# Exponentials written over the logits in PSUM, with a copy for GpSimd's sum

## The chip, the cores and the metric

The kernel runs on one core of a Trainium2 chip. A core has TensorE (PE, matmuls), VectorE (DVE), ScalarE (ACT), GpSimd (POOL) and SyncE (SP, which issues the DMAs). They run side by side, each through its own queue in order, and wait for each other by semaphores. SBUF is the working memory that all of them reach; PSUM holds what matmuls write, and of the other engines only VectorE and ScalarE read or write it. The metric is the device time of one execution in microseconds. Profiles count from the first to the last instruction, the span.

## What is computed

One layer that mixes three groups of heads over 2048 positions of width 1024: forgetting attention (6 heads of 64), a chunked mLSTM (4 heads of 96), and cross-attention to 256 memory tokens (4 heads of 64). All take their inputs from one projection, go through a gate and an output projection, and a layer norm ends it. The change touches the two attentions:

```python
logits = einsum('bhqd,bhkd->bhqk', q_blk, kh) + c_blk[..., :, None] - c[..., None, :]
p = softmax(where(causal, logits, -inf), axis=-1)
return einsum('bhqk,bhkd->bhqd', p, vh)
```

In the cross-attention the logits are `q @ mem_k` alone, without a mask.

## The kernel before, in words

*Precision.* Matmuls run in a rounded 32-bit format (`F32R`). To keep more digits, a value `x` is split into a rounded `h` and the rest `l = x - h`. A projection is three matmuls for each piece of 128 rows (`h,h`, `l,h` and `h,l`), and the weights of attention, which are exponentials, are split as well: `ph` is rounded, `pl` the rest, and each is multiplied by the values `v`.

*Attention.* An item is one head with a block of 512 queries; there are 40. `att_max` finds each query's largest logit: matmuls into a PSUM tile `mx`, and VectorE's maxima of it into `mp`. `att_qk` makes the logits, 128 keys at a time (a chunk): two matmuls into a PSUM tile `st`, `st<-qm,km` and `st<-qb,kb`, the keys on the partitions and up to 512 queries along them, with the maximum already subtracted. Items of the second half of the positions have 12 or 16 chunks, others 2, 4 or 8. There are 272 chunks in all. `att_exp` (lines 604 to 624) then does for each chunk:

- ScalarE writes `ph`, the rounded exponential of `st`
- ScalarE writes `p`, the full exponential of `st`, to SBUF; `st` is free then
- VectorE writes `pl = p - ph`
- GpSimd adds `p` to the item's sum `acc` over the chunks (the softmax's denominator); the item's first chunk has no addition, its `p` is `acc` itself

`att_pv` multiplies: `o<-ph,v` and `o<-pl,v`, both adding into one PSUM tile `o`. `att_end` divides by the sum and stores the block.

*Around it.* TensorE's other work fills in between: the projections (`pj<-h,h`, `pj<-l,h`, `pj<-h,l`, listed in `SEQ`), later the mLSTM units (`ml_unit`, 16 of them, tile names `mq`, `mk`, `vv`, `dd`, `cst`, `vw`, `kr`) and the output tiles (`out_tile`, `pj<-h,yh` and so on), for which the output weights `wo` are loaded.

*What sets the order.* The class `Machine` is a planner. Each part of the work is a generator that asks for buffers (`Alloc`) and yields instructions. The planner keeps a clock for each engine by costs of its own, and issues next, on the engine that can start earliest, the ready instruction with the lowest number in `PRIO`. So the order on each engine is fixed when the program is made, and a change of a few lines can move instructions everywhere behind it. Buffers are counted by tag: two of `st`, two of `p`, two of `ph`, three of `pl`, one of `o`; `ph` and `pl` can also use the four of `ta`. The loader of weights has the lowest number of all and takes a `raw` buffer or, where none is free, a `p` (`RAW`).

Nearly all instructions are recorded by the planner's `issue`, so the profile puts them on line 204 and they are told apart by the names of their tiles.

## Time and profile before

| | |
|---|---|
| time, median of 3 runs | 1445.92 us (1445.73 to 1448.08) |
| the profiled execution | 1446.53 us, its span 1444.8 us |
| granted clock of TensorE, mean | 0.987 |
| attention's logits | from 74 us to 1124 us of the span |
| last projection, first output matmul | 1172 us, 1189 us |
| HBM read and written | 97.62 MB and 44.00 MB, 98 GB/s over the span |

A row of a group reads: line, engine, operation, tiles written and read, shapes, count | busy us, mean ns of one | idle time of the engine just before them and what ended it. The mean ns is the length of one instruction. Where instructions follow each other without a wait, the next begins before the one before it ends, so their pitch is shorter than that length. A row of a timeline has the start, the length, the engine and the instruction. PEld is the loading of a matmul's weights, which runs beside the matmul before it.

### The profile page before, as it was taken

The numbers are of one execution on the slowest core, as the hardware profiler recorded it, in microseconds if no ns is written. First come the engines' busy times: TensorE is split into PE (matmuls) and PEld (weight loads), VectorE is DVE, ScalarE is ACT, GpSimd is POOL, SyncE is SP. The second block draws the span as 40 slices with busy tenths as digits, with TensorE's granted clock in tenths as the row PEclk, the third lists the DMA queues.
The fourth block names the chain that finished last, engine by engine and source line by source line (L and its number), as shares of the span: only waits on it lengthen the run. The fifth ranks groups of instructions, "written<-read, shape, count | busy, mean of one in ns | idle before, by whom it ended". The sixth has DMA issues, their size and how long they took to land.

```text
span 1444.8 us, 22963 instructions
## 1 busy us (share of the span) xinstructions
PE 1355.7 (94%) x7904; PEld 1160.5 (80%) x7904; DVE 1058.8 (73%) x2158; ACT 673.1 (47%) x1463; POOL 435.0 (30%) x401
## 2 busy tenths in 40 slices
PE   6999999999999999999999989999998969989998
PEld 6888998998877798977787768787686757877886
DVE  5887356637588979579797788779889786767455
ACT  5444234424355643344646364544636566555100
POOL 2011002303043201013737071722726314445300
PEclk9999999999999999999999999999999979999999
DMA  6613232231322452431011402131111586765432
GB/s 200 205 46 103 79 109 86 78 115 56 116 74 74 143 177 61 131 105 54 21 49 53 121 9 61 38 104 56 58 40 56 165 239 200 216 185 160 134 134 92
DMA packets 123556, 151.81 MB, mean 105 GB/s; under 512 B 16832, under 2 KB 72080, under 8 KB 123440
## 3 DMA queue, kind: packets, MB, share of 16 engines
q1 hardware_dynamic: 123440, 150.35, 34.9%
q8 instruction: 63, 1.03, 0.3%
q14 instruction: 53, 0.43, 0.1%
HBM read 97.62 MB, written 44.00 MB: 98 GB/s over the span
## 4 chain that ended last, share of the span: by engine, by line
PE 56%; DVE 19%; POOL 6%; ACT 6%; issue 4%; DMA 3%; SPq 0%; DVEq 0%; POOLq 0%; ACTq 0%
PE pj L204 44%; POOL acc L204 6%; PE mx L204 5%; DVE pl L204 5%; PE st L204 4%; PE o L204 3%; DVE cv L204 2%; DVE mp L204 1%; ACT p L204 1%; DVE l L204 1%; DMA raw<-in_wo_dram 1%; DVE sc L204 1%; DVE y L204 1%; DVE mx L204 1%; DMA raw<-in_wg_dram 1%
## 5 line engine op out<-in xcount | busy, mean ns | idle before, releaser
L204 POOL TENSOR_TENSOR acc<-acc,p 128x512 f32<-128x512 f32 (+2 forms) x232 | 326.0, 1405 | 611.4 <-PE mx L204 223.1
L204 PE MATMUL pj<-h,h 128*128 128x288 f32 (+3 forms) x1496 | 488.5, 327 | 14.8 <-ACT h L204 8.0
L204 PE MATMUL pj<-l,h 128*128 128x288 f32 (+3 forms) x1496 | 480.4, 321 | 0.9 <-DVE l L204 0.9
L204 PE MATMUL pj<-h,l 128*128 128x288 f32 (+3 forms) x1496 | 479.3, 320 | 0.3 <-DVE l L204 0.2
L204 PEld LDWEIGHTS pj<-h,h 128*128 128x128 f32 x1496 | 284.1, 190 | 34.2 <-ACT h L204 8.2
L204 PEld LDWEIGHTS pj<-l,h 128*128 128x128 f32 x1496 | 284.3, 190 | 25.1 <-DVE l L204 2.2
L204 PEld LDWEIGHTS pj<-h,l 128*128 128x128 f32 x1496 | 283.5, 189 | 19.5 <-DVE l L204 0.7
L204 DVE TENSOR_TENSOR pl<-p,ph 128x512 fp32r<-128x512 f32 (+2 forms) x191 | 196.7, 1034 | 27.5 <-ACT p L204 20.8
L204 DVE TENSOR_TENSOR l<-raw,h 128x512 fp32r<-128x512 f32 (+2 forms) x174 | 123.1, 728 | 61.8 <-ACT h L204 58.0
L204 ACT ACTIVATE p<-st 128x512 f32<-128x512 f32 (+2 forms) x232 | 126.9, 547 | 65.7 <-POOL acc L204 32.2
L204 ACT CAST h<-raw 128x512 fp32r<-128x512 f32 (+2 forms) x174 | 107.4, 632 | 98.6 <-DMA raw<-in_wg_dram 67.8
L204 ACT ACTIVATE ph<-st 128x512 fp32r<-128x512 f32 (+2 forms) x231 | 127.7, 554 | 51.3 <-PE st L204 47.7
L204 PE MATMUL o<-pl,v 128*128 128x512 f32 (+2 forms) x268 | 110.6, 414 | 31.7 <-DVE pl L204 29.3
L204 PE MATMUL st<-qb,kb 128*128 128x512 f32 (+2 forms) x272 | 110.0, 404 | 0.0
L204 DVE TENSOR_REDUCE mp<-mx 128x1 f32<-128x512 f32 x144 | 95.1, 684 | 19.2 <-PE mx L204 18.4
L204 PE MATMUL pj<-h,yh 128*128 128x512 f32 (+1 forms) x264 | 106.6, 404 | 0.3 <-DVE dd L204 0.2
L204 PE MATMUL mx<-km,qm 66*128 66x512 f32 (+2 forms) x304 | 97.4, 359 | 6.9 <-DVE mp L204 2.8
L204 PE MATMUL st<-qm,km 68*128 68x512 f32 (+2 forms) x272 | 103.1, 379 | 0.9 <-ACT p L204 0.9
L204 PE MATMUL pj<-h,ylo 128*128 128x512 f32 (+1 forms) x264 | 102.6, 389 | 0.0
L204 PE MATMUL pj<-l,yh 128*128 128x512 f32 (+1 forms) x264 | 102.4, 388 | 0.0
L204 PEld LDWEIGHTS o<-pl,v 128*128 128x128 f32 x268 | 51.0, 191 | 63.7 <-DVE pl L204 59.5
L204 PE MATMUL o<-ph,v 128*128 128x512 f32 (+2 forms) x231 | 87.5, 379 | 0.0
(180 smaller groups left out, 1910.2 us busy)
## 6 DMA issues: line engine op xcount, KB each, us to landing
raw<-in_wg_dram SPq DMA_DIRECT2D x80, 256.0 KB
raw<-in_wg_dram SPq DMA_DIRECT2D x32, 288.0 KB
raw<-in_xt_dram SPq DMA_DIRECT2D x32, 256.0 KB
yr<-y_scr SPq DMA_DIRECT2D x32, 256.0 KB
xr<-in_x_dram SPq DMA_DIRECT2D x32, 256.0 KB
out_dram<-xr SPq DMA_DIRECT2D x32, 256.0 KB
qk_scr<-cv SPq DMA_DIRECT2D x24, 256.0 KB
qb<-qm SPq DMA_DIRECT2D x40, 128.0 KB
```

The lines of the kernel that those rows point to most:

```text
L204: op.fn(*op.args, **op.kw)
```

## The change

The second exponential is no longer written to `p` in SBUF but over the logits in `st`. A new thread, `att_low`, takes the subtraction: VectorE reads the full exponential from `st` and `ph` from SBUF. ScalarE then copies `st` to `p`, from which GpSimd adds as before. `st` is freed when both the copy and the subtraction have been issued (`free_st` counts them).

```diff
-        yield ACT.activation(p_[:, 0:nq], st[:, 0:nq], AF.Exp)
-        free(st)
-        pl = yield Alloc(("pl", "ta"), [P, BLK], F32R)
-        yield DVE.tensor_tensor(pl[:, 0:nq], p_[:, 0:nq], ph[:, 0:nq].bitcast(F32), op=ALU.subtract)
-        it["w"][ci] = (ph, pl)
+        yield ACT.activation(st[:, 0:nq], st[:, 0:nq], AF.Exp)
+        spawn(att_low(it, ci, st, ph, nq), PRIO["qk"])
+        yield ACT.copy(p_[:, 0:nq], st[:, 0:nq])
+        free_st(st)
...
+    def free_st(st):
+        nm = st.tensor.name
+        st_left[nm] = st_left.get(nm, 2) - 1
+        if not st_left[nm]:
+            free(st)
+
+    def att_low(it, ci, st, ph, nq):
+        pl = yield Alloc(("pl", "ta"), [P, BLK], F32R)
+        yield DVE.tensor_tensor(pl[:, 0:nq], st[:, 0:nq], ph[:, 0:nq].bitcast(F32), op=ALU.subtract)
+        free_st(st)
+        it["w"][ci] = (ph, pl)
```

The planner's order changes with it. ScalarE's queue in one of the long heads (16 chunks, second half of the positions), before; the names in brackets are the engines whose semaphore is waited for, and `ta` is a buffer used for `ph`:

```order
L204 ACTIVATE ph_10005<-st_9991 128x512 [waits PE_49]
L204 ACTIVATE p_10006<-st_9991 128x512 [waits DVE_49,Pool_49]
L204 ACTIVATE stg_10024<-pj_9894 128x96 [waits DMAHW2_49]
L204 ACTIVATE ta_10012<-st_10007 128x512 [waits PE_49]
L204 ACTIVATE p_10016<-st_10007 128x512 [waits DVE_49,Pool_49]
```

The same two chunks' rows with the change:

```order
L204 ACTIVATE ph_10234<-st_10213 128x512 [waits DVE_49,PE_49]
L204 ACTIVATE st_10213<-st_10213 128x512
L204 COPY p_10235<-st_10213 128x512 [waits Activation_49,Pool_49]
L204 ACTIVATE ph_10249<-st_10237 128x512 [waits DVE_49,PE_49]
L204 ACTIVATE st_10237<-st_10237 128x512
L204 COPY p_10250<-st_10237 128x512 [waits Activation_49,Pool_49]
```

The wait for a free `p` (GpSimd's semaphore) has moved from the second exponential to the copy, which also waits for ScalarE's own exponential before it.

TensorE's queue at that place, before (`st` are logits, `o` the products with the values):

```order
L204 MATMUL st_9991<-qm_108,km_107 128x512
L204 MATMUL st_9991<-qb_9495,kb_9457 128x512
L204 MATMUL o_9907<-pl_9986,v_9382 128x512
L204 MATMUL st_10007<-qm_108,km_107 128x512
L204 MATMUL st_10007<-qb_9495,kb_9457 128x512
L204 MATMUL o_9907<-ph_9989,v_9382 128x512
L204 MATMUL o_9907<-pl_10002,v_9382 128x512
L204 MATMUL st_10020<-qm_108,km_102 128x512
```

And with the change (`pj` are projections):

```order
L204 MATMUL st_10213<-qm_108,km_107 128x512
L204 MATMUL st_10213<-qb_9655,kb_9617 128x512
L204 MATMUL o_10106<-ph_10209,v_9531 128x512
L204 MATMUL pj_10218<-h_9300,h_6076 128x288
L204 MATMUL pj_10218<-l_9301,h_6076 128x288
L204 MATMUL pj_10218<-h_9300,l_6077 128x288
L204 MATMUL o_10106<-pl_10229,v_9531 128x512
L204 MATMUL st_10237<-qm_108,km_107 128x512
L204 MATMUL st_10237<-qb_9655,kb_9617 128x512
```

Projection matmuls now stand between the products with `ph` and with `pl`, and the next logits stand behind the product with `pl`.

TensorE's queue where attention ended before; the last product `o<-pl` of the last head is followed by projections, and the first mLSTM unit (`mq,mk`) stands among them:

```order
L204 MATMUL o_12549<-pl_12833,v_11018 128x512
L204 MATMUL pj_12823<-h_5693,h_11940 128x512
L204 MATMUL pj_12823<-l_5694,h_11940 128x512
L204 MATMUL pj_12823<-h_5693,l_11941 128x512
L204 MATMUL mx_12861<-ident_r,acc_12555 128x128 x4
```

With the change, from the last projection on:

```order
L204 MATMUL pj_13049<-h_6151,l_12566 128x512
L204 MATMUL pj_13154<-mq_13059,mk_13060 128x128 x4
L204 MATMUL pj_13173<-ident_r,mk_13060 128x96 x4
L204 MATMUL pj_13199<-vv_13062,dd_13061 128x97 x4
L204 MATMUL pj_13214<-cst_166,mq_13059 128x97 x2
L204 MATMUL pj_13214<-cst_167,mq_13059 128x97 x2
L204 MATMUL pj_13219<-vw_13063,kr_13064 96x97 x4
L204 MATMUL pj_13289<-mq_13137,mk_13138 128x128 x4
L204 MATMUL pj_13300<-ident_r,mk_13138 128x96 x4
L204 MATMUL o_12960<-ph_13078,v_11285 128x512
L204 MATMUL o_12960<-pl_13298,v_11285 128x512
L204 MATMUL st_13308<-qm_108,km_107 128x512
```

The projections are over here, and most chunks of the last head stand behind them and behind the first mLSTM unit. In ScalarE's queue the casts of 13 `wo` loads stand between this head's chunks.

## The prediction

> **What bounds the kernel now.** I read the page first, then the list of waits, then stretches of the span by window, then the groups with shapes kept apart.

> ```profile
> PE 1355.7 (94%) x7904; PEld 1160.5 (80%) x7904; DVE 1058.8 (73%) x2158; ACT 673.1 (47%) x1463; POOL 435.0 (30%) x401
> ...
> PE 56%; DVE 19%; POOL 6%; ACT 6%; issue 4%; DMA 3%; SPq 0%; DVEq 0%; POOLq 0%; ACTq 0%
> ```

> TensorE (PE) is busy 94% of the span and holds 56% of the chain that ended last. The matmuls do not change, so the change can only win back time in which PE waits, 1444.8 - 1355.7 = 89 us and what the modelled ends hide. VectorE holds 19% of the chain, so I look for what PE waits for on VectorE.

> ```profile
> PEld o L204 <- DVE pl L204: 59.5, 94, 2.2
> ...
> PE o L204 <- DVE pl L204: 29.3, 48, 2.0
> ```

> The list of waits (total, times, longest). PE waits for `pl`, the subtraction that the change moves, 29.3 us with its matmuls and 59.5 us with its weight loads; part of the latter is covered by a matmul still running. I take the loss as **45 us**, the middle.

> ```profile
> 831.00:867.00 36.00, 31.96 (x153) 24.36 (x152) 30.39 (x40) 23.40 (x48) 28.76 (x20) 0.95 0.03 9
> ...
> 831.00:867.00 36.00, 9.81 (x22) 4.16 (x21) 22.73 (x22) 0.95 0.03 9
> ```

> A dense stretch of attention, all engines first (length; busy time of PE, PEld, DVE, ACT, POOL), then `pl` alone (PE, PEld, DVE). 22 chunks in 36 us are 1.64 us each. GpSimd is busy 28.8 of 36 us, VectorE 30.4, ScalarE only 23.4. So GpSimd's sum and the subtraction set the pace.

> ```profile
> L204 POOL TENSOR_TENSOR acc<-acc,p 128x512 f32<-128x512 f32 x160 | 255.9, 1599 | 441.0 <-PE mx L204 176.8 <-PE o L204 88.4 <-ACT p L204 86.9
> ...
> L204 DVE TENSOR_TENSOR pl<-p,ph 128x512 fp32r<-128x512 f32 x129 | 137.7, 1072 | 24.2 <-ACT p L204 18.2 <-PE pj L204 1.2 <-PE st L204 1.0
> ...
> L204 DVE TENSOR_TENSOR pl<-p,ph 128x256 fp32r<-128x256 f32 x38 | 29.8, 785 | 2.7 <-ACT p L204 2.1
> ...
> L204 DVE TENSOR_TENSOR pl<-p,ph 128x384 fp32r<-128x384 f32 x24 | 29.4, 1224 | 0.6 <-ACT p L204 0.5
> L204 DVE TENSOR_TENSOR pl<-p,ta 128x512 fp32r<-128x512 f32 x31 | 29.2, 943 | 1.6 <-ACT p L204 0.6
> ...
> L204 DVE TENSOR_TENSOR pl<-acc,ph 128x512 fp32r<-128x512 f32 x39 | 26.5, 679 | 6.7 <-ACT acc L204 6.6
> ...
> L204 POOL TENSOR_TENSOR xr<-xr,lb 128x512 f32<-128x512 f32 x16 | 22.2, 1390 | 1.3
> ...
> L204 DVE TENSOR_TENSOR ylo<-st,yh 128x512 fp32r<-128x512 f32 x32 | 20.8, 677 | 0.6 <-ACT yh L204 0.4 <-issue 0.3
> ...
> L204 DVE TENSOR_TENSOR v<-pj,v 128x256 fp32r<-128x256 f32 x26 | 10.9, 418 | 20.2 <-ACT v L204 20.1
> ```

> The same subtraction takes 1072 ns in most chunks but 679 ns in a head's first chunk (`pl<-acc`), for which GpSimd adds nothing. With one operand in PSUM (`ylo<-st`) it takes 677 ns, also where GpSimd works. The two engines slow each other when both read two SBUF operands.

> **The change, part by part.** *Subtraction.* VectorE saves (1072-679)x129 + (943-679)x31 + (785-418)x38 + (1224-550)x24 = 89 us of busy time; 550 lies between the other two sizes. GpSimd's addition should fall from 1.60 to about 1.39 us. Neither is a gain by itself.

> [...]

> *Copies.* 232 on ScalarE.

> ```profile
> L204 ACT ACTIVATE p<-st 128x512 f32<-128x512 f32 x160 | 96.4, 603 | 41.9 <-DVE pl L204 28.9 <-POOL acc L204 12.4
> ...
> L204 DVE TENSOR_TENSOR y<-y,zs 128x256 f32<-128x256 f32 x40 | 24.7, 618 | 1.1
> ...
> L204 ACT COPY ot<-o 128x512 f32<-128x512 f32 x40 | 23.5, 586 | 56.3 <-PE o L204 55.0 <-DVE y L204 1.3
> ...
> L204 ACT COPY ot<-mx 128x256 f32<-128x256 f32 x40 | 15.1, 376 | 25.3 <-PE mx L204 24.8
> ```

> 200 of 586 ns, 24 of some 480, 48 of 376: 147 us more ScalarE busy time (47% to 57%).

> ```profile
> 601.00 0.37 ACT L204 CAST v<-pj 128x256 fp32r<-128x256 f32 x1 [4.46 <-PE pj L204]
> ...
> 601.41 0.42 DVE L204 TENSOR_TENSOR v<-pj,v 128x256 fp32r<-128x256 f32 x1 [4.41 <-ACT v L204]
> ...
> 601.92 0.39 ACT L204 ACTIVATE tz<-pj 128x256 f32<-128x256 f32 x1 [0.54 <-DVE v L204]
> ...
> 838.91 0.30 PE L204 MATMUL pj<-h,h 128*128 128x288 f32 x1
> 839.04 0.29 PE L204 MATMUL pj<-l,h 128*128 128x288 f32 x1
> ...
> 839.71 0.40 PE L204 MATMUL o<-ph,v 128*128 128x512 f32 x1
> 839.95 0.28 PE L204 MATMUL st<-qm,km 68*128 68x256 f32 x1
> ...
> 1124.17 0.60 ACT L204 ACTIVATE ph<-st 128x512 fp32r<-128x512 f32 x1
> 1124.65 0.61 ACT L204 ACTIVATE p<-st 128x512 f32<-128x512 f32 x1
> ```

> The timeline: start, length. Independent ScalarE instructions follow each other every 0.48 us, and 512-column matmuls every 0.24, projection matmuls of 288 every 0.13. The copy reads what the exponential before it writes and must wait for its end plus some 0.03 us (`y<-y,zs`, 1.1 us over 40). **ScalarE per chunk: 0.48 + 0.60 + 0.03 + 0.48 = 1.59 us**, nearly the old pace of 1.64.

> *The added wait.* `tz` and `v` above only read one PSUM tile, and still `tz` waits 0.54 us until VectorE's read is over: readers on two engines go one after the other. Counted over the program's semaphore values, the subtraction waits in 241 of 272 chunks for the **copy**, which stands ahead of it and itself waits for GpSimd to free `p`. From the first exponential to the end of `pl` it was 0.48 + 0.60 + 0.06 + 1.07 = 2.21 us and becomes 0.48 + 0.60 + 0.03 + 0.59 + 0.06 + 0.68 = 2.44 us. Behind the copy queue the next chunk's exponentials, behind the subtraction VectorE's maxima, and PE waits for both. The two `st` banks are held longer too: `pl`, then the PV matmul, then the logits of the chunk after next (0.06 + 0.24 + 0.24 + 0.40 + 0.06) and again 2.44 are 3.44 us for two chunks, **1.72 us each**.

> [...] Were the reads free to overlap, the loop would be 1.41 us and ScalarE's 1.59 would decide: 9 us lost in the two poor heads below and none elsewhere, about 1416.

> *Unknown cost.* No row shows ScalarE writing PSUM.

> ```profile
> L204 DVE TENSOR_REDUCE mp<-mx 128x1 f32<-128x512 f32 x144 | 95.1, 684 | 19.2 <-PE mx L204 18.4
> ...
> L204 DVE CUSTOM_DVE_ANT_0 mx<-mx,mrow 128x512 f32<-128x512 f32 x24 | 17.0, 708 | 1.6 <-PE mx L204 1.4
> ```

> VectorE's masked maximum, which also writes PSUM, takes 24 ns more than the plain one. So I bound the exponential by 0.586 (the fastest such row) and 0.627 us, and take 0.60; the ends are worth -4 and +6 us over 232.

> *The order.* PE's order thins out the dense heads: in the 12 long heads (168 chunks) 749 instead of 537 projection matmuls stand between a head's first and last logits, 100 maxima in both. Two heads of 16 chunks keep few, 12 and 36. There PE has 0.96 + 0.14 for maxima + 0.10 or 0.30 = 1.20 or 1.40 us a chunk against the loop's 1.72: 16x0.52 + 16x0.32 = 13 us lost. The other 136 chunks have 0.96 + 0.14 + 0.69 = 1.79 us, just enough; I charge 0.1 us each for other ScalarE work in between, 14 us. **Waits for `pl`: 27 instead of 45, -18 us.**

> ```profile
> L204 PE MATMUL pj<-h,h 128*128 128x288 f32 (+3 forms) x1496 | 488.5, 327 | 14.8 <-ACT h L204 8.0
> ...
> L204 PE MATMUL mx<-km,qm 66*128 66x512 f32 (+2 forms) x304 | 97.4, 359 | 6.9 <-DVE mp L204 2.8
> ```

> Maxima behind a shorter subtraction: half of 6.9, **-3 us**. Projections wait 8.0 us for ScalarE's casts; a third more, **+3 us**.

> *End of attention.* Projections now end before the last head does: some 11 chunks have no projections between them.

> ```profile
> 1128.00:1189.00 61.00, 46.32 (x275) 39.69 (x273) 46.83 (x124) 40.58 (x103) 11.52 (x13) 0.86 0.71 203
> 1172.00:1189.00 17.00, 10.89 (x67) 9.84 (x65) 15.13 (x43) 13.39 (x36) 4.51 (x5) 0.71 0.82 236
> ...
> 1160.79 4.67 DMA raw<-in_wo_dram
> ...
> 1169.77 6.43 DMA raw<-in_wo_dram
> ```

> Before, from the last PV matmul to the first output matmul (1128 to 1189), PE lost 61.0 - 46.3 = 15 us; 17 us of the stretch lay behind the last projection, and the last two rows are waits for `wo` on the chain there. The loader takes `p` buffers ahead of the exponentials, so now the last head halts until 13 `wo` loads are through. Two `raw` and two `p` hold four loads at a time: some three batches of 4.7 to 6.4 us, 16 us. Then 11 chunks of at most 1.72 us, 19 us, and half of the old 17, since some mLSTM units now run under the last head: 44 us with about 23 us of matmuls (11 x 0.96, and 12 for units and transposes, an estimate), a loss of 21. **+6 us.** DMAs, their sizes and the matmuls' number stay; SP's rows only move with the order.

> **Sum:** -18 - 3 + 3 + 6 = -12 us. The profiled execution took 1446.5 (span 1444.8 and 1.7 around it), 0.6 over the median of the runs, 1445.9: **1434**, its own range 1424 to 1442.

> **Rivals.** *The fillers cover all.* The 136 chunks lose nothing, only the two poor heads their 13 us: -32 - 3 + 3 + 6 = -26, **1420**. For it speak 1.79 us of matmuls against a loop of 1.72; against it the readers in a row. Chance 0.2.

> *ScalarE takes GpSimd's place.* The change then doesn't do what it says: the subtraction, queued behind a copy that waits for GpSimd, comes as late as ever. With 1.59 or 1.72 against 1.64 us between half of the dense gain and none of it is left: 1443 to 1452, about **1447**. Chance 0.17.

> *Slower: the last head.* If its halt lasts four batches of 6.4 us, 26 us, and the mLSTM units' ScalarE work in between delays the chunks by 8 more, the end costs 18 us on top: **1452**. It decides from 56 us between the last projection and the first output matmul. For it speak the ScalarE rows there, in which the units' work stands between the chunks; against it, that ScalarE was busy only 40.6 of 61 us before. Chance 0.15.

> *Slower: latency.* If half of the 168 chunks pay the longer 2.44 us in full (0.23 x 84 = 19 us), the dense gain is gone: **1453**. For it speaks that PE waited in 94 of 272 cases already; against it, the filler. Chance 0.08.

> **How the numbers follow.** My forecast has 0.4. Some 3 us, 0.2%, is what a measurement of this kernel can tell from no change. Faster: 0.4 + 0.2 and a little of the third, 0.61. Same: most of the third, 0.16. Slower: the last two, 0.23. The range goes 7 us below the best case and 3 us above the worst, for the unknown price of the write to PSUM: 1413 to 1456.

> **What would show it.** `pl` at about 680 ns for 512 columns, the sum near 1.4 us; ScalarE over 800 us busy; PE's waits for `pl` at about 60% of before; a copy's row just before each `pl`; 40 to 50 us from the last projection to the first output matmul. It is wrong if `pl` stays above 1 us, if PE's waits for `pl` do not fall, or if the last stretch exceeds 56 us.

## The result, and the profile after

The changed kernel takes **1499.36 us** (median of 4 runs, 1496.12 to 1503.11) against 1445.83 us before (median of 4): ratio 1.037, 95% interval 1.0338 to 1.0402. Slower by 54 us, where 12 us less was forecast. The profiled execution took 1503.11 us, its span 1501.4 us; TensorE's mean granted clock was 0.956 (0.987 before).

Busy time and count of instructions of each engine, after:

```profile
PE 1398.5 (93%) x7904; PEld 1185.6 (79%) x7904; DVE 966.2 (64%) x2158; ACT 799.7 (53%) x1735; POOL 380.6 (25%) x401
```

VectorE lost 93 us of busy time (89 forecast), ScalarE gained 127 (147 forecast), GpSimd lost 54. PE is still 93% busy, and its busy time rose by 43 us with the same 7904 matmuls: 132 us of this execution ran at half clock, 37 us of the one before, and there the matmul behind a 512-column one of the logits starts 0.43 us after it in place of 0.23. The groups of the changed instructions, shapes kept apart:

```profile
L204 POOL TENSOR_TENSOR acc<-acc,p 128x512 f32<-128x512 f32 x160 | 210.3, 1314 | 548.5 <-ACT p L204 526.3 <-PE pj L204 12.9 <-PE o L204 5.2
...
L204 DVE TENSOR_TENSOR pl<-st,ph 128x512 fp32r<-128x512 f32 x200 | 137.3, 688 | 135.8 <-ACT p L204 116.8 <-ACT acc L204 9.2 <-ACT st L204 4.4
...
L204 ACT ACTIVATE st<-st 128x512 f32<-128x512 f32 x200 | 120.1, 601 | 0.1
...
L204 ACT COPY p<-st 128x512 f32<-128x512 f32 x160 | 93.8, 586 | 14.2 <-DVE pl L204 4.3 <-ACT st L204 0.7 <-DVE tail L204 0.2
```

The subtraction fell from 1072 to 688 ns, the sum from 1599 to 1314, and the exponential written to PSUM costs 601 ns. All three prices lie near the forecast. The waits (total, times, longest) do not:

```profile
DVE pl L204 <- ACT p L204: 158.0, 146, 3.2
...
PEld o L204 <- DVE pl L204: 68.5, 109, 2.0
...
PE o L204 <- DVE pl L204: 29.7, 47, 1.6
```

PE waits for `pl` as long as before (59.5 and 29.3 us then), although `pl` takes a third less time. VectorE in its turn waits 158 us for the copy `p`, which it does not read.

The busy share and the granted clock of PE in 40 slices of the span, after:

```profile
PE   7999999999999999999998989899999779898998
...
PEclk9999999999999999999995999889999779999999
```

and the clock before:

```profile
PEclk9999999999999999999999999999999979999999
```

One slice stands at 0.5 and there are dips at 0.8 and 0.7; slice 22 (788 to 826 us) is one head. To see where the time went I cut each profiled execution at the first exponential of each of the twelve long heads (items 28 to 39) and took from each piece what its matmuls take at full clock (the median pitch of the same matmul in the kernel before, 1296 us in all). What is left is PE's loss. Worked out from the traces, in us:

| | before | after |
|---|---|---|
| start, up to item 28 | 42.2 | 53.4 |
| nine long heads | 40.1 | 41.5 |
| items 31, 35 and 39 | 18.1 | 69.1 |
| from the last chunk of item 39 to the end | 48.2 | 41.2 |
| sum | 148.6 | 205.2 |

The difference of the two sums is that of the two profiled executions. **51 of the 57 us lie in three heads**: 6.6 became 24.1 in item 31, 5.3 became 20.4 in item 35, 6.2 became 24.6 in item 39. These are the heads from which the new order took the projections, the bare heads from here on: between the first and the last product of the head stand 0, 15 and 36 projection matmuls, where 60, 60 and 45 stood; the other nine have 42 to 99. Item 31 up to the next head, before and then after (length; busy time of PE, PEld, DVE, ACT, POOL; clock):

```profile
763.00:825.00 62.00, 58.18 (x313) 48.02 (x311) 47.10 (x73) 28.26 (x57) 22.01 (x15) 1.00 0.35 99
```

```profile
784.00:853.00 69.00, 60.74 (x223) 43.89 (x221) 37.54 (x73) 35.41 (x72) 17.88 (x15) 0.78 0.29 80
```

The same head takes 7 us more with 90 matmuls fewer, at a clock of 0.78.

### The profile page after: what moved, and what is told of

Same layout as the page of the kernel before. It is cut to its first block, busy times and chain, and to the rows that moved or that the text cites. A ratio compares the mean times of both kernels' runs of the same rounds, so it can differ in the third digit from the quotient of the medians.

```text
span 1501.4 us, 23256 instructions
## 1 busy us (share of the span) xinstructions
PE 1398.5 (93%) x7904; PEld 1185.6 (79%) x7904; DVE 966.2 (64%) x2158; ACT 799.7 (53%) x1735; POOL 380.6 (25%) x401
## 5 line engine op out<-in xcount | busy, mean ns | idle before, releaser
L204 PE MATMUL pj<-h,h 128*128 128x288 f32 (+3 forms) x1496 | 489.8, 327 | 12.7 <-ACT h L204 9.7
L204 PE MATMUL pj<-l,h 128*128 128x288 f32 (+3 forms) x1496 | 482.5, 323 | 1.7 <-DVE l L204 1.6
L204 PE MATMUL pj<-h,l 128*128 128x288 f32 (+3 forms) x1496 | 481.4, 322 | 0.2 <-DVE l L204 0.2
L204 POOL TENSOR_TENSOR acc<-acc,p 128x512 f32<-128x512 f32 (+2 forms) x232 | 272.0, 1172 | 740.6 <-ACT p L204 628.6
L204 PEld LDWEIGHTS pj<-h,h 128*128 128x128 f32 x1496 | 285.9, 191 | 34.0 <-ACT h L204 10.5
L204 PEld LDWEIGHTS pj<-l,h 128*128 128x128 f32 x1496 | 286.2, 191 | 27.5 <-DVE l L204 3.0
L204 PEld LDWEIGHTS pj<-h,l 128*128 128x128 f32 x1496 | 285.3, 191 | 19.5 <-DVE l L204 0.4
L204 DVE TENSOR_TENSOR pl<-st,ph 128x512 fp32r<-128x512 f32 (+2 forms) x272 | 170.5, 629 | 178.7 <-ACT p L204 158.0
L204 ACT ACTIVATE ph<-st 128x512 fp32r<-128x512 f32 (+2 forms) x272 | 150.5, 553 | 97.7 <-PE st L204 91.3
L204 DVE TENSOR_TENSOR l<-raw,h 128x512 fp32r<-128x512 f32 (+2 forms) x174 | 125.1, 737 | 60.3 <-ACT h L204 56.8
L204 ACT CAST h<-raw 128x512 fp32r<-128x512 f32 (+2 forms) x174 | 107.9, 631 | 96.8 <-DMA raw<-in_wg_dram 64.4
L204 ACT ACTIVATE st<-st 128x512 f32<-128x512 f32 (+2 forms) x272 | 150.3, 553 | 0.1
L204 PE MATMUL o<-pl,v 128*128 128x512 f32 (+2 forms) x272 | 120.5, 448 | 30.9 <-DVE pl L204 29.7
L204 ACT COPY p<-st 128x512 f32<-128x512 f32 (+2 forms) x232 | 123.2, 531 | 20.3 <-DVE pl L204 4.8
L204 PE MATMUL o<-ph,v 128*128 128x512 f32 (+2 forms) x272 | 111.2, 409 | 4.9 <-ACT ph L204 4.9
L204 PE MATMUL st<-qb,kb 128*128 128x512 f32 (+2 forms) x272 | 115.5, 425 | 0.0
L204 PEld LDWEIGHTS o<-pl,v 128*128 128x128 f32 x272 | 54.0, 200 | 72.8 <-DVE pl L204 68.5
L204 PE MATMUL st<-qm,km 68*128 68x512 f32 (+2 forms) x272 | 108.8, 400 | 1.8 <-DMA qm<-rr 1.0
L204 PE MATMUL pj<-h,yh 128*128 128x512 f32 (+1 forms) x264 | 107.2, 406 | 0.7 <-ACT n L204 0.7
L204 PE MATMUL mx<-km,qm 66*128 66x512 f32 (+2 forms) x304 | 98.9, 364 | 7.9 <-DVE mp L204 4.2
L204 DVE TENSOR_REDUCE mp<-mx 128x1 f32<-128x512 f32 x144 | 95.1, 684 | 16.7 <-PE mx L204 16.0
L204 PE MATMUL pj<-h,ylo 128*128 128x512 f32 (+1 forms) x264 | 103.2, 391 | 0.0
```

Source lines behind the costliest of these rows:

```text
L204: op.fn(*op.args, **op.kw)
```

## Experiments

The first question was whether the order, the instructions or the clock makes the loss. In e1, e3, e11, e13, e14 and e17 every engine's instructions stand in the order of the changed kernel, in e2 and e18 in that of the kernel before, apart from what is said. e6 has the order of e5; e10, e12 and e15 have that of e9. The others are planned anew, and their order moves.

**e1_order: the new order with the old instructions.**

```diff
-        yield ACT.activation(st[:, 0:nq], st[:, 0:nq], AF.Exp)
+        yield emits(ACT.activation(st[:, 0:nq], st[:, 0:nq], AF.Exp),
+                    lambda: nc.scalar.activation(p_[:, 0:nq], st[:, 0:nq], AF.Exp))
...
-        yield ACT.copy(p_[:, 0:nq], st[:, 0:nq])
+        yield emits(ACT.copy(p_[:, 0:nq], st[:, 0:nq]), lambda: None)
```

`emits` lets the planner plan one instruction and issues another in its place; the subtraction reads `p_`.

> The changed kernel's order of instructions with the old instructions: the second exponential goes to p in SBUF, the subtraction reads p, there is no copy. Theory A (order: the new order takes the projections out of three heads of 16 chunks, TensorE waits for pl there and its granted clock halves): most of the 54 us stay, 1480 to 1500, with over 90 us at half clock in the profiled run (132 in the changed kernel, 37 before). Theory B (instructions: the copy's load on ScalarE, or the subtraction queued behind it, costs the time): 1440 to 1455 and about 40 us at half clock.

1489.21 us, ratio 1.0298 (1.0279 to 1.0318). The new order with the old instructions costs 43 us. The loss in items 31, 35 and 39 is 58.6 us (18.1 before), in the other nine 39.4. The half-clock time is only 80 us (1486.5 x 2 x (1 - 0.973)), less than theory A asked for.

**e2_load: the old order with one more ScalarE copy in each chunk**, `nc.scalar.copy(idle[:, 0:nq], st[:, 0:nq])` behind the second exponential.

> The old kernel in its old order with one more ScalarE copy of 128x512 from st to an unused tile in each of the 272 chunks, so ScalarE's busy time rises by some 150 us as in the changed kernel, and nothing else. Theory A (order): 1446 to 1455, since ScalarE has 47% of the span to itself. Theory B in the form 'ScalarE's load': over 1475.

1456.3 us, 1.0076 (1.0061 to 1.0091): 10 us, just over what A allowed. Part of it is not ScalarE's load: the copy is one more reader of `st`, and PE's next logits wait for it:

```profile
PEld st L204 <- ACT idle L618: 33.9, 78, 0.9
...
PE st L204 <- ACT idle L618: 7.8, 24, 0.5
```

**e3_warm: zero matmuls in the three heads.**

```diff
+                    for _ in range(2):
+                        nc.tensor.matmul(o[:, q0:BLK], zero, ph[:, 0:nq], start=False, stop=False)
```

> The changed kernel with two matmuls more behind each o<-ph of three heads (items 31, 35 and 39, 48 chunks): a tile of zeros times ph, added into o. 96 matmuls of 512 columns, 23 us at full clock. Theory A in its strong form (the halved clock is what stretches these heads): TensorE stays busy while it waits for pl, the clock stays up, 1465 to 1485. Rival (the chain from the exponentials to pl sets the pace of these heads, the clock only follows): the matmuls lie in the wait, no gain, 1497 to 1510, though the half-clock stretches shrink.

1490.65 us, 1.0315 (1.0291 to 1.034). 9 us faster with 96 matmuls more, and 78 us at half clock (1494.4 x 2 x (1 - 0.974)) in place of 132. Item 31:

```profile
782.00:844.00 62.00, 56.64 (x248) 41.37 (x248) 37.23 (x75) 34.49 (x71) 17.95 (x15) 1.00 0.31 90
```

At full clock this head takes 62 us in place of 69. So the halved clock costs 7 us here and some 9 us in the kernel. Theory A's strong form falls: the clock is a part, not the cause. 54 us less at half clock are worth 9 us, because PE then waits or multiplies zeros instead. The timeline shows what sets the pace (start, length; chunks of item 31 at full clock):

```profile
795.29 0.60 ACT L204 ACTIVATE ph<-st 128x512 fp32r<-128x512 f32 x1
...
795.78 0.59 ACT L204 ACTIVATE st<-st 128x512 f32<-128x512 f32 x1
...
796.46 0.59 ACT L204 COPY p<-st 128x512 f32<-128x512 f32 x1
...
796.96 0.60 ACT L204 ACTIVATE ph<-st 128x512 fp32r<-128x512 f32 x1
...
797.08 0.69 DVE L204 TENSOR_TENSOR pl<-st,ph 128x512 fp32r<-128x512 f32 x1 [1.19 <-ACT p L204]
...
797.83 0.51 PE L204 MATMUL o<-pl,v 128*128 128x512 f32 x1 [0.21 <-DVE pl L204]
...
798.75 0.69 DVE L204 TENSOR_TENSOR pl<-st,ph 128x512 fp32r<-128x512 f32 x1 [0.97 <-ACT p L204]
```

The subtraction starts 0.03 us after the copy's end (797.05), not after its own exponential's end (796.37). From the first exponential to the end of `pl` it is 2.48 us (795.29 to 797.77), and the chunks follow each other every 1.67 us here, 1.77 over the head. Without the halved clock this is the forecast's loop of 1.72.

**e4_wo: the loads of the output weights take no `p` buffers.** `Alloc(RAW if ncol <= BLK and k <= wo_box["first"] else "raw", ...)` in the loader.

> The changed kernel, but the output weights' loads may no longer take p buffers, so that the last head does not halt for them. Theory C (the halt of the last head and the end of attention are the loss): from the last projection to the first output matmul 45 us or less instead of 58, time 1480 to 1487. Theory A (order, three unfilled heads): two of the three heads are as before, 1488 to 1500.

1487.16 us, 1.0283 (1.0266 to 1.03): 12 us faster, item 39's loss 17.3 in place of 24.6. But from the last projection to the first output matmul it is 65 us (1169.6 to 1234.6), not 45. The last head loses some 7 us less without the halt, and that distance says nothing about it. The order moved a little with this edit, so the other 5 us are not taken apart.

**e5_spread to e8_spread_swap: projections spread over the heads.** A generator of projections goes on only while

```diff
+        return (it is None or it["i"] < 28 or it["next"] == len(it["chunks"])
+                or pace["used"] < 1 + 0.8 * it["next"])
```

> The changed kernel with its instructions; only the planner lets projections into a head of the second half at a rate, 0.8 groups of three matmuls for each chunk of the head that has begun, so that between the first and the last product of the twelve long heads stand 33 to 60 projection matmuls in place of 0 to 99. Theory A (the heads without fillers are the loss): PE's loss in items 31 and 35, 24 and 20 us in the changed kernel, falls to the 7 and 5 of before, and the last head's falls too: 1458 to 1470. Rival (the longer chain to pl slows every head, and the fillers taken from the rich heads are missed there): 1490 or more.

1501.69 us, 1.0383 (1.0357 to 1.0409): no gain. The loss moved: the three heads fell from 69.1 to 36.8 us, the other nine rose from 41.5 to 67.8. The rival was right. The fillers are a fixed stock, and every head has a loop longer than its own matmuls: one in which PE's own work is 0.87 us a chunk at a pitch of 1.77, as item 31, wants the other 0.90 from somewhere else.

> The order of e5_spread with the old instructions (second exponential to p in SBUF, subtraction from p, no copy). If the order is all that matters, the same time as e5_spread within 3 us. If the added copy costs what the unused copy cost in e2_load, 10 us less than e5_spread, about 1450. If the faster subtraction is worth something once every head has fillers, e5_spread is the faster of the two.

1492.1 us, 1.0323 (1.0301 to 1.0346): 10 us under e5, as e1 lies 10 us under the changed kernel. The new instructions cost 10 us more than the old ones in either order; the faster subtraction is not seen.

> e5_spread, and the output weights' loads no longer take p buffers as in e4_wo. If the last head's halt still costs anything with fillers in it: 5 to 12 us less than e5_spread. If the spread fillers have covered it: the same within 3 us.

1516.95 us, 1.0496 (1.0472 to 1.0521). Neither answer: item 39's loss fell to 7.1, but the end rose from 49.6 to 67.9.

> e5_spread with the subtraction issued ahead of the copy, so that the copy waits for the subtraction and not the other way round (order otherwise nearly the same). If the subtraction's wait for the copy is what keeps PE waiting for pl: 5 to 15 us less than e5_spread. If ScalarE's queue matters more (its copy now holds it for 0.7 us per chunk, behind which stand the next exponentials): 5 us or more above e5_spread.

1577.61 us, 1.0921 (1.0896 to 1.0945). The second answer, far more strongly than written. The copy now waits for the subtraction, and ScalarE stands still meanwhile:

```profile
DVE pl L204 <- ACT st L204: 204.6, 153, 2.5
ACT p L204 <- DVE pl L204: 140.4, 185, 2.6
```

So one of the two readers waits in either order. That it is worse where the waiting engine has the next exponentials behind it is likely, but not shown: against the expectation, the planner's order moved with this edit too, some 1000 of PE's 7904 matmuls among it.

**e9_hold and e10_hold_inst: a planner that does not know of the copy.** e9 is the old kernel with `free(st)` moved behind the subtraction. e10 issues in the place of its second exponential

```diff
+            nc.scalar.activation(st[:, 0:nq], st[:, 0:nq], AF.Exp)
+            nc.scalar.copy(p_[:, 0:nq], st[:, 0:nq])
```

and subtracts from `st`.

> The old kernel and its instructions, but st is freed only when the subtraction has been issued, as in the changed kernel; the planner does not know of a copy. Its order keeps 27 to 66 projection matmuls in each of the twelve long heads (24 to 63 before). Theory L (holding st until the subtraction closes a loop through the two banks, and the order that follows from it puts the next logits behind the product with pl): 1470 to 1490, a loss of 2 to 5 us more than before in nearly every long head. Theory F (only the fillers' place in the order matters): 1444 to 1452.

1473.21 us, 1.0189 (1.0166 to 1.0212). In the time theory L, in the heads theory F: the twelve heads lose 56.4 us together (58.2 before), items 31, 35 and 39 only 16.4. The whole difference lies after attention, which neither theory named:

```profile
1133.00:1218.00 85.00, 62.63 (x350) 56.62 (x349) 57.03 (x170) 50.59 (x139) 16.29 (x19) 0.74 0.71 196
```

From the last product of attention to the first output matmul PE loses 85.0 - 62.6 = 22 us, where it lost 15 before, and more behind it: the loss after attention is 70.6 us against 48.2. It shows that holding `st` longer does not by itself make heads bare; what else is new in the plan does, the copy or the subtraction's own thread `att_low`. Nor does it put the logits behind the product with `pl`, as theory L has it: those of the chunk after next stand ahead in 138 of 144 chunks. It also shows how much a small move of the order can do at the end.

> The order of e9_hold with the changed kernel's instructions: exponential over st, copy to p right behind it, subtraction from st; the planner plans with the old costs, so no head loses its fillers. If the order that came from the planned copy is the loss and the instructions are worth what e2_load showed: 10 us above e9_hold, 1455 to 1462 under theory F. If the longer chain costs in itself: 20 us or more above e9_hold and over 1475. If the faster subtraction pays once the order is kept: at or below e9_hold.

1507.73 us, 1.0437 (1.0395 to 1.0479): 35 us over e9, the answer "the longer chain costs in itself". No head is bare here (the three lose 17.7 us), yet the start loses 65.6 us (46.2 in e9) and the other nine heads 55.8 (40.0). In this order PE waits for `pl` at another place, the next logits, because `st` is not free before:

```profile
PEld st L204 <- DVE pl L622: 87.5, 127, 2.4
...
PE st L204 <- DVE pl L622: 43.2, 81, 2.0
```

**e11 to e14: what of the copy costs.** First the two orders without copies and sums. The copy is issued only for a head's first chunk, and GpSimd's addition is planned but not issued.

> The changed kernel in its order, without the copies to p and GpSimd's additions in all chunks but a head's first, so the denominators hold the first chunk alone. The subtraction then waits for its own exponential only. If the order is the larger part of the loss and the copies cost some 10 us as in e2_load: 1480 to 1490, with most of the loss in items 31, 35 and 39 still there. If the subtraction's wait behind the copy is what stretches those heads (two-bank loop 1.43 us without it, by 2.44 less 0.59 for a chunk): their loss falls to about half, 1455 to 1475.

1442.6 us, 0.9982 (0.9965 to 0.9999): **57 us less than the changed kernel**, more than either answer. The waits for `pl` are what I had forecast for the change:

```profile
PEld o L204 <- DVE pl L204: 37.6, 64, 1.9
...
PE o L204 <- DVE pl L204: 15.3, 33, 1.4
```

Their middle is 26 us (27 in the forecast). The nine heads lose 14.8 us (40.1 before, 41.5 after); the three bare heads still lose 47.6.

> e10_hold_inst without the copies to p and GpSimd's additions in all chunks but a head's first (denominators of the first chunk alone). If the copy, with the subtraction behind it, makes the 34 us between e10_hold_inst and e9_hold: 1468 to 1478, at e9_hold. If the exponential written to PSUM, or the longer hold of st, makes them: 1495 or more. If the shorter subtraction pays when nothing stands before it: under 1468.

1430.69 us, 0.9894 (0.9878 to 0.9911): the third answer, 77 us under e10 and 43 under e9. Items 31 and 35 run at a pitch of 1.36 us. How much of this is the shorter subtraction and how much GpSimd's missing sum is not parted.

Copies and sums went together in these two. The next pair, in the order of after again, parts them: e13 leaves out only the additions; e14 lets each later copy go from a constant in SBUF to an unused tile (`nc.scalar.copy(idle[:, 0:nq], mrow[:, 0:nq])`).

> The changed kernel in its order with all its copies to p, but without GpSimd's additions (denominators hold a head's first chunk alone), so no copy waits for a free p. If the cost of 57 us between e11_no_copy and the changed kernel is the copies' wait for GpSimd (c): 1443 to 1455. If it is the copy itself and the subtraction behind it (a and b): 1490 to 1500.

1476.96 us, 1.0218 (1.0203 to 1.0233), and the waits

```profile
DVE pl L204 <- ACT p L204: 159.8, 153, 3.0
...
PEld o L204 <- DVE pl L204: 58.8, 95, 1.9
...
PE o L204 <- DVE pl L204: 24.1, 45, 1.5
```

> As e13_no_sum, but each copy of a later chunk reads a constant tile in SBUF and writes an unused one: ScalarE has the same number of instructions in the same places, and the subtraction waits for its own exponential only (denominators as in e13_no_sum). If the subtraction's wait behind the copy (a) is the cost: 1443 to 1455. If ScalarE's time (b) is: as e13_no_sum within 5 us.

1446.86 us, 1.0009 (0.9998 to 1.0021), and the waits

```profile
DVE pl L204 <- ACT st L204: 119.3, 139, 2.8
...
PEld o L204 <- DVE pl L204: 42.3, 69, 1.9
...
PE o L204 <- DVE pl L204: 17.9, 39, 1.4
```

The 57 us are therefore 4 us of ScalarE's time (e11 to e14), **30 us because the copy reads `st`** (e14 to e13) and 22 us with GpSimd's sum (e13 to after). The step from e14 to e13 leaves the number of instructions and their places alone. What it changes is who waits: the subtraction stands behind the copy, and the next logits behind both. The copy also stands behind the end of its own exponential, 0.03 us after it where the unrelated copy starts 0.08 us before it; the first wait is by far the longer.

The traces show what this does to a chunk. From the start of the first exponential to the end of `pl` the chunks of 512 columns in the twelve long heads take, as a median of 132, 1.81 us in e11 (1443 us in all), 1.82 in e14 (1447), 2.43 in e13 (1477) and 2.48 in the changed kernel (1499); e1, in the same order with the old instructions, has 2.25 (1489). **The kernel before has 3.29 us, and still takes only 1446.** So the chain is not longer than it was; what it holds up has changed. Before, `st` is free after the second exponential, and the logits of the chunk after next stand ahead of the product with `pl` in PE's queue in 139 of 144 chunks of the long heads (a head's last two have none after next). In the new order (e1 and e5 too) they stand behind it in all 144, so the chain sets the pace wherever PE's other work does not cover it.

**e15_dve_sum and e16_dve_spread: no copy, VectorE adds the sum from PSUM.**

```diff
+            nc.vector.tensor_tensor(pl[:, 0:nq], st[:, 0:nq], ph[:, 0:nq].bitcast(F32), op=ALU.subtract)
+            if ci:
+                nc.vector.tensor_tensor(acc_[:, q0:BLK], acc_[:, q0:BLK], st[:, 0:nq], op=ALU.add)
```

> The order of e9_hold; exponential over st, VectorE subtracts from st and then adds st to the head's sum itself, ScalarE copies only a head's first chunk, GpSimd adds nothing. Nothing is left out. VectorE gets 232 additions of some 0.68 us, about 150 us, behind 89 us saved in the subtraction. If the copy was the whole cost: between e12_hold_no_copy and before, 1435 to 1445. If VectorE, now some 1120 of 1440 us busy, sets the pace: 1455 to 1480.

1491.69 us, 1.0316 (1.0296 to 1.0336). Over both answers: `st` is held until the addition is over, and PE waits for that.

```profile
PEld st L204 <- DVE acc L621: 69.9, 120, 1.4
...
PE st L204 <- DVE acc L621: 28.6, 73, 1.0
```

> As e15_dve_sum, but planned as such (the planner knows of VectorE's additions) and with the projections let in at 0.8 groups per chunk as in e5_spread, so that the long heads keep 30 to 54 projection matmuls each. If the order of e9_hold loses its 22 us at the end of attention only by its own accident: 5 to 20 us under e15_dve_sum. If the spread order loses in every head as e5_spread did: above e15_dve_sum.

1483.14 us, 1.026 (1.0245 to 1.0275), 9 us under e15 as the first answer has it; but the end loses 69.4 us here too, so not for the reason given there. The start lost 35.3 us in place of 54.7. No version with the whole sum beat the kernel before.

**e17_p4 and e18_before_p4: four `p` buffers in SBUF in the same order**, `bufs=4 if a.tag == "p" else BUFS[a.tag]`.

> The changed kernel with four p buffers in SBUF in place of two; the planner still counts two, so every engine's order is the same. If the 22 us between e13_no_sum and the changed kernel are the copies' wait for GpSimd to free a p: 1475 to 1483. If GpSimd slows the others in another way: 1495 or more.

1498.72 us, 1.0381 (1.0358 to 1.0404): no change. The 22 us of GpSimd's sum are not the copies' wait for a free `p`; the changed kernel's list of waits has no wait of the copy for GpSimd either.

> The kernel before with four p buffers in place of two, its order unchanged. Its second exponential waits 29 us for GpSimd to free a p (12 of them in the chunks of 512 columns). If that wait reaches PE as in the changed kernel: 1432 to 1441, a kernel faster than both. If PE's other work covers it: 1443 to 1447.

1459.08 us, 1.0093 (1.0068 to 1.0118): slower than without, outside both answers. So taking that wait away gains nothing here; why the kernel is 15 us slower without it stays open.

## Why the prediction was wrong

*What the operations cost:* right. Subtraction 688 ns (about 680), GpSimd's sum 1.31 us (near 1.4), the exponential to PSUM 601 ns (0.60), ScalarE 799.7 us busy (over 800, so just under; the sum of its prices, 147 more, would have been 820). The forecast speaks of 232 copies, but its sum counts 272, which is what the kernel has: 40 of them write a head's first `acc`. Reading `st` from PSUM the subtraction took 688 ns, `pl<-acc` in the kernel before, from SBUF alone, 679: 9 ns more.

*The loop:* right as a length. Forecast 2.44 us from exponential to `pl` and 1.72 us a chunk; 2.48 and 1.77 were measured in item 31 at full clock. What it was compared with is wrong: the forecast has 2.21 us for the kernel before, worked out without waits, and the trace 3.29. Nor do the rows show that GpSimd's sum and the subtraction set the pace of the dense stretch: PE is the busiest engine there (31.96 of 36 us).

***The step that failed** is "Waits for `pl`: 27 instead of 45, -18 us".* After the change their middle is 49. That is hardly more than before; most of the 57 us stands in PE's busy time, which rose by 43 us with the half clock. The step rested on two sizes, and both were off.

- The added wait. I priced the subtraction's place behind the copy at 0.23 us a chunk, the difference from the old chain, and let other matmuls cover it everywhere but in two heads. The new order had put the logits of the chunk after next behind the chain, and against the same order without a second reader the copy lengthens the chain by 0.61 us (1.82 to 2.43). As a reader of `st` it costs 30 us (e14 to e13), 11.5 us of it in the nine filled heads and 14.5 in the bare ones. Without copy and sum the forecast's 27 came true (26).
- The bare heads. "16x0.52 + 16x0.32 = 13 us" took PE's own work in them as 1.20 and 1.40 us a chunk; in item 31 it is 0.87, for the maxima that I spread evenly are not there. The third such head, the last one, I put into the end of attention. Three heads cost 51 us more than before. That the order makes them bare is shown by e1 (58.6 us there with the old instructions) and e9 (16.4 with another order).

*The granted clock* was not considered at all. In item 31 it was halved twice, each time after 3.41 us in which PE was busy for 0.45 and 0.64 of them; over the 69 us it was 0.78, and the loop of 1.77 us, measured in e3 at 1.00, took 2.02. By e3 this is some 9 us of the 54.

*Maxima and projections:* the waits behind `mp` went from 2.8 to 4.2 us and not down, those for the casts from 8.0 to 9.7. Both are small.

*End of attention:* 44 us from the last projection to the first output matmul were forecast, 58.5 measured (1177.9 to 1236.4). That is past the 56 of the rival "the last head", and the last head did cost 18 us more, but what follows cost 7 less: together 11, where 6 was forecast. That 18 is also this rival's figure is luck, for it laid it to the halt. By e4 the halt for `wo` is some 7 us, and the distance itself does not decide.

*The rivals.* "Latency" (1453) came nearest to the mechanism, a chain that the fillers do not cover, and priced it at 19 us; copy and sum cost 57. "ScalarE takes GpSimd's place" named the copy ahead of the subtraction, but foresaw only that the gain would be lost. "The fillers cover all" fell. That the readers of one PSUM tile went one after the other was rightly taken for the loop (in e3's rows the subtraction starts 0.03 us after the copy's end); the forecast then used it only where the heads had few fillers.

*Still open:* why GpSimd's sum costs 22 us (e13 to after). It is not the number of its buffers (e17). One part the traces suggest: with the sum the copy waits for GpSimd's semaphore besides its own exponential's, and ScalarE has a semaphore instruction between the two in 170 chunks (10 in e13, 130 in e17), although it does not wait for GpSimd there. From the exponential's end to the copy's start are 77 ns as a mean (32 in e13, 65 in e17), over 232 chunks some 10 us of chain (an estimate); no run tests what of it reaches PE. Also, without the sum some VectorE rows that read SBUF were shorter, here one with two operands in e13

```profile
L204 DVE SCALAR_TENSOR_TENSOR cv<-u,cw_sb,cv 128x512 f32<-128x512 f32 x72 | 53.8, 749 | 3.1 <-ACT cv L204 1.7
```

against 832 ns in the changed kernel. Rows with one operand were shorter too (`u<-tail`, three columns, 160 ns against 335), so the forecast's "both read two SBUF operands" is not the whole of it. VectorE was 32 us less busy; that this reaches PE is not shown. The 22 us by which e9 and the kernels like it lose more after attention are open too.

## What to carry to other kernels

A tile in PSUM with readers on two engines was a queue here (1.82 us a chunk became 2.43 when the copy read `st` too): price the second reader as standing behind the first, in every chunk and not only where PE is short of other work, and price the tile as held until the last reader is done. Ask first what stands behind the chain in the matmul engine's queue: 3.29 us cost little where the logits of the chunk after next stood ahead of it, and 2.48 us much where they stood behind. Where a planner orders the work, a change of costs moves the fillers, and fillers are a fixed stock: compare, head by head, the loop's length with PE's own work between the loop's ends, and add the halved clock where it falls short (7 us in item 31, where PE's own work was 0.87 of 1.77 us). To part an added instruction's time from the waits it brings, keep it in its place and let it read something else.
